# Fewer weight-sum transfers in the mixer's last stages, more in the MLP, and a last matrix part that reads all its weight sums from the scratch

## The chip, the cores and the metric

The kernel runs on one core of one Trainium2 chip. The metric is the device time of the whole program in microseconds (us), the median of several executions; lower is better. The five engines of the core are named as in the profile: PE (matmul; PEld is its weight load), DVE (vector), ACT (scalar), POOL (GpSimd) and SP (here only an issuer of transfers). ACT, POOL and SP each issue transfers on a queue of their own, and the 16 DMA engines of the core carry them.

## The reference, cut to what matters

Two layers, each a mixer (attention and mLSTM side by side) and then a squared-ReLU MLP, on 512 tokens of width 1024:

```python
h = rmsnorm(x, norm_mix); z = h @ w_in          # mixer: attention, mLSTM, gates
mixed = sigmoid(g_a) * (att @ w_att_branch) + sigmoid(g_m) * (hm @ w_m_branch)
x = x + mixed @ w_out
u = relu(rmsnorm(x, norm_ffn) @ w_ff1)          # MLP: 1024 -> 4096
x = x + (u * u) @ w_ff2                         #      4096 -> 1024
```

All of it is float32. The change touches how the weights of the MLP, `w_ff1` and `w_ff2`, reach the matmuls, and nothing that is computed.

## The kernel before, in words

**Matmuls in split precision.** Every operand is split into a high and a low part (`wh`, `wl` for weights, `uh`, `ul` for activations): ACT makes the high part by a copy that rounds, DVE subtracts it to get the low part. Three matmuls (`mm3`: high·high, high·low, low·high) stand for one.

**The MLP by Strassen's scheme.** The MLP is cut into four parts of 1024 hidden columns. Part 0 of the first matrix is done plainly (class `Plain`). The other products take seven block products in place of eight (numbered 1, 5, 6, 3, 7, 2, 4 in the order of work), with sums of weight blocks as operands. `first(part, i, u)` makes the hidden activations, `second(part, u)` multiplies them by `w_ff2` and adds the results to `x` (`gain`, one DVE instruction for each 128x512 block, reading a PSUM bank and freeing it). Each block product of `second` is a slot of two units (24 matmuls of 128x512 in all), each of `first` a slot of one unit; there are 102 units in a layer, in the order of the list `slots`, and the split weights are prepared `SPL` = 5 units ahead (`prepare`). Part 3's `second` comes last and has no `first` slots between its own.

**Weight sums by transfers.** The four sums that the scheme needs (D, A, B, C) can be made by the DMA engines in a scratch in DRAM: a "copy" (`Sums.copy`, issued by ACT, line 400) puts one block there, an "add" (`Sums.add`, issued by POOL, line 405) accumulates a second one onto it. B adds D, and C adds B, so these come later. Each copy and add moves half a matrix block, 512 KB. The scratch then holds the sum, and SP loads it like any weight. For `w_ff1` all four sums come this way; for `w_ff2` only D does, and `weights(which, h)` in `second` makes the others on the way with `plus` (DVE, line 925), in place on the loaded raw tile.

**When the transfers go out.** `plan_sums` lists the copies and adds of a layer as `jobs` (64 in a layer), and each `beat` takes the next job. Beats stand at fixed places of the mixer's stages (`beats(...)` beside `weave`), and in the MLP after units with `i % 5 in (1, 3)`. A copy is tied by `issue_after` to the last weight split on ACT; an add is tied to a small POOL copy (`mark`, line 403) that reads that split. The program's scheduler places them in the engines' instruction streams by these ties.

**Buffers around the change.** The loads of `second` go to four raw buffers (`raw2`, tags `p` and `q` for each half `h`); a load waits until the last reader of its buffer is done. Loads of `first` (`load1`, line 948) share three raw buffers. `w_m_branch`, the mixer's last but one weight, and `w_out`, its last, go through `chunk` (line 182 for the load, 192 and 193 for the split), with three raw buffers.

Of the kernel before, what the change touches and what calls it, by code (L numbers as in the profile page):

```python
# [19 lines left out]
D = 1024  # L20
KT = D // P
# [14 lines left out]
def hybrid_kernel(ctx, tc, x, norm_mix, w_in, att_q_norm, att_k_norm, att_sinks, m_gate_bias,  # L36
# [84 lines left out]
    def g_mix(l, k):  # L121
        return gcol[:, 8 * l + k:8 * l + k + 1]

    def g_ffn(l, k):
        return gcol[:, 16 + 8 * l + k:17 + 8 * l + k]
# [128 lines left out]
    def weave(fill, side=()):  # L254

        side = sorted(side, key=lambda e: e[0])
        at = 0.0
        for width, f in fill:
            while side and side[0][0] <= at + 1e-6:
                side.pop(0)[1]()  # L260
            f()
            at += width
        for _, f in side:
            f()
# [76 lines left out]
    norm = norm0 = Norm(lambda k: g_mix(0, k))  # L341
# [32 lines left out]
    jobs, sums = [], {}  # L374
# [38 lines left out]
    def plan_sums(l):  # L413

        s = [None] + [Sums(l, part, w1_rows) for part in range(1, 4)]
        p = [Sums(l, part, w2_rows, "D") for part in range(4)]
        sums.clear()
        sums.update({(1, part): s[part] for part in range(1, 4)})
        sums.update({(2, part): p[part] for part in range(4)})
        jobs.extend(s[1].copies("DABC") + s[1].adds("DAB") + p[0].copies("D") + s[1].adds("C")  # L420
                    + s[2].copies("DABC") + p[0].adds("D") + s[2].adds("DAB") + p[1].copies("D") + s[2].adds("C")
                    + s[3].copies("DABC") + p[1].adds("D") + s[3].adds("DAB") + p[2].copies("D") + s[3].adds("C")
                    + p[3].copies("D") + p[2].adds("D") + p[3].adds("D"))

    def beat():
        if jobs:
# [2 lines left out]
    def beats(*at):  # L429
        return [(a, beat) for a in at]  # L430

    def mixer(l, norm, late, order, phase):
# [319 lines left out]
        def ev_v(b, ps):  # L752
            if b == 0:
# [6 lines left out]
        side = [(0, lambda: k_vec(0)), (0, lambda: q_vec(0)), (0, lambda: k_vec(1)), (0, lambda: q_vec(1)),  # L760
                (7 - 1.25, lambda: k_tr(0)), (7 - 1.75, lambda: q_tr(0))]
# [100 lines left out]

        side += [(57.75 + 1.25 * f, lambda f=f: head_tr(f)) for f in range(MH)]
        plan_sums(l)
        side += beats(*(2.5 * n for n in range(1, 17)), *(42 + 1.5 * n for n in range(14)))
        weave(feat_steps(acts, wcols(C_QM, 512), ev_qk) + s0 + s1 + tok_steps(acts, wcols(C_VM, 512), ev_v)
              + a_steps(0, g0) + a_steps(1, g1) + s2 + tok_steps(acts, wcols(C_OM, 512), ev_o) + s3, side)
        sgm = [g2, g3]
# [1 line left out]
        for g in range(2):  # L870
            def ev_m(m, ps, g=g):
                i = 4 * g + m
                ve.tensor_tensor(sgm[g][m], sgm[g][m], ps, op=ALU.mult)
                ve.tensor_tensor(prod[i], prod[i], sgm[g][m], op=ALU.add)
                mixed[i] = split(prod[i])

            weave(feat_steps(hmT, lambda k, g=g: [w_m_branch[l, k * P:(k + 1) * P, 512 * g:512 * g + 512]], ev_m),
                  beats(1.0, 2.5))


        norm = Norm(lambda k: g_ffn(l, k))
# [10 lines left out]
    def mlp(l, norm, late, phase):  # L892
# [18 lines left out]
        def w_split(r):  # L911

            with tc.high_priority():
                hi, lo = (spl.tile(list(r.shape), F32R, tag=t, name=nm(t)) for t in ("wh", "wl"))
                last_wh[:] = sc.activation(hi, r, AF.Copy), hi[:, 0, :]  # L915
                ve.tensor_tensor(lo, r, f32(hi), op=ALU.subtract)  # L916
            return hi, lo
# [44 lines left out]
        def second(part, u):  # L962

            a11, a12, a21, a22 = (u[i][:, :, H * t:H * (t + 1)] for t in range(2) for i in range(2))
            s = uraw.tile([P, 4, H], F32, tag="s", name=nm("s"))
            end = part == 3
            b11, b12, b22, b21 = ([None] * 2 for _ in range(4))
            ps = {}

            def load(to, tag, h, src):  # L970
                with tc.high_priority():
                    to[h] = raw2.tile([P, 2, T], F32, tag=f"{tag}{h}", name=nm("raw"))
                    nc.sync.dma_start(to[h], src.rearrange("(k p) n -> p k n", p=P))

            def block(i, j, h):
                return w2_rows(l, part, i, j, h)

            def weights(which, h):
                if which == 1:
                    load(b11, "p", h, block(0, 0, h))  # L980
                    load(b12, "q", h, block(0, 1, h))
                    r = w_split(b11[h])
                    plus(b11[h], b11[h], b12[h])
                elif which == 5:
                    load(b22, "q", h, block(1, 1, h))
                    r = w_split(b11[h])
                    plus(b11[h], b11[h], b22[h])
                elif which == 6:
                    r = w_split(b11[h])
                elif which == 3:  # L990
                    r = w_split(b22[h])
                elif which == 7:
                    load(b12, "q", h, sums[2, part].to("D", h))
                    r = w_split(b12[h])
                elif which == 2:
                    load(b21, "q", h, block(1, 0, h))
                    r = w_split(b21[h])
                    plus(b21[h], b21[h], b11[h])
                else:
                    r = w_split(b21[h])  # L1000
                return r

            def left(which):
                if which == 5:
                    minus(s, a22, a21)
                elif which == 6:
                    minus(s, s, a11, -1.0)
                elif which == 3:
                    minus(s, s, a12, -1.0)
                elif which == 7:  # L1010
                    minus(a21, a11, a21)
                return {1: a11, 2: a12, 4: a22, 7: a21}.get(which, s)

            def slot(which, bank, fresh, gains):

                ws, a = {}, []

                def prep(h):
                    ws[h] = weights(which, h)

                def run(h):
                    if h == 0 and fresh:
                        ps[bank] = banks(bank)
                    (hi, lo), (ah, al) = ws[h], a[0]
                    for kt in range(2 * h, 2 * h + 2):
                        for i in range(2):
                            c = slice(i * P, (i + 1) * P)
                            mm3(ps[bank][:, i, :], ah[:, kt, c], al[:, kt, c], hi[:, kt % 2, :], lo[:, kt % 2, :],
                                fresh and kt == 0, False, skip_group_check=True)

                return Slot([lambda: prep(0), lambda: prep(1)], [lambda: run(0), lambda: run(1)],
                            lambda: [gain(t, j, ps[bank], g, d) for t, j, g, d in gains],
                            lambda: a.append(u_split(left(which))))

            x_, y_ = "xy" if part % 2 == 0 else "yx"
            z_ = "f" if end else y_
            return [slot(1, x_, True, [(0, 0, 1, False)]), slot(5, y_, True, [(1, 1, -1, False)]),
                    slot(6, x_, False, [(0, 1, -1, False)]), slot(3, y_, False, [(0, 1, -1, end)]),
                    slot(7, x_, False, [(1, 1, -1, end)]), slot(2, z_, True, [(0, 0, 1, end)]),
                    slot(4, x_, False, [(1, 0, 1, end)])]  # L1040
# [100 lines left out]
        class Plain:  # L1141
# [5 lines left out]
            def load(self, h):  # L1147
                self.w[h] = load1(w_ff1[l, T * h:T * (h + 1), self.c0:self.c0 + H])
# [21 lines left out]
        plain = [Plain(0, 0, "f"), Plain(0, 1, "x")]  # L1170
        for h in range(2):
            for f in plain:
                f.load(h)
        weave([(0.5, lambda k=k, f=f: f.step(k)) for k in range(KT) for f in plain], late + [(6.5, norm.inverse)])
        for f in plain:
            f.evac(us[0])
        us.append(new_u(1))
# [24 lines left out]
        def go(i, s, n):  # L1202
            if i == 0:
                s.before()
            prepare(i + SPL)
            at = slots.index(s) + 1
            if n == 0 and at < len(slots):
                slots[at].before()
            s.runs[n]()
            if n == len(s.runs) - 1:  # L1210
                s.done()
            if i % 5 in (1, 3):
                beat()

        weave([(1.0 if i >= len(units) - 4 else 0.0, lambda i=i, s=s, n=n: go(i, s, n))
# [3 lines left out]
    late = ([(0.75 + 0.9 * (k - 2), lambda k=k: norm.turn(k)) for k in range(2, KT)]  # L1219
            + [(6.5, lambda: gains(grow, 16))]  # L1220
            + [(3.0 + 2.0 * j, lambda j=j: norm.squares(j)) for j in range(2)])
    order = None
    for l in range(DEPTH):
        with ExitStack() as phase:
            norm = mixer(l, norm, late, order, phase)
        late = norm.steps(1, 1.5, 0.5)
        with ExitStack() as phase:
            norm = mlp(l, norm, late, phase)
        late = norm.steps(0, 1.5, 0.5) if norm else []
# [41 lines left out]
```

## Time and profile before

| | before |
|---|---|
| median of 3 executions | 1349.47 us (1347.91 to 4564.59) |
| profiled execution, whole | 1353.9 us |
| its span, first to last instruction | 1352.2 us |
| PE busy | 1307.2 us, 97% of the span |
| DVE busy | 970.2 us, 72% |
| ACT busy | 763.0 us, 56% |
| bytes moved by DMA | 219.58 MB |
| copies into the scratch / adds | 64 / 64, 512 KB each |

The page is read from PE outward: PE is busy nearly all of the span, so time can be lost only in its few gaps and where its clock is lower (the granted clock, 0.992 over the span). The other engines matter where PE waits for them. Windows of the span show where the gaps are; the chain that ended last and the waits show what ended them.

### The profile page before, as it was taken

The page shows a single profiled execution, that of the slowest core. Times are in us where ns is not written, and L with a number is a line of the kernel's source. Part 1 is how long each engine was busy: PE and PEld are TensorE (multiplying, and loading weights), DVE is VectorE, ACT ScalarE, POOL GpSimd, SP SyncE. Part 2 cuts the span into 40 slices and gives each one's busy share as a digit, 9 for nine tenths or more (in the row PEclk, how much of TensorE's full clock was granted, in tenths as well). Part 3 has the DMA queues.
Part 4 walks back from the last instruction along what each step waited for, and adds up shares of the span by engine and source line. Part 5 has one row for each costly group of instructions (what it writes and reads, how often), then busy time and mean ns, then how long its engine had stood idle before and what let it go on. Part 6 is the DMA issues. An engine that isn't in the chain of part 4 may idle for free. (4 is left out here: it accounts for less than half of the span.)

```text
span 1352.2 us, 19313 instructions
## 1 busy us (share of the span) xinstructions
PE 1307.2 (97%) x6966; PEld 1107.0 (82%) x6966; DVE 970.2 (72%) x1505; ACT 763.0 (56%) x1367; POOL 204.9 (15%) x347
## 2 busy tenths in 40 slices
PE   8999999979999999999999999999999999999998
PEld 6877788868889989998778777888788898898977
DVE  4688764566568797978847887645746678879796
ACT  5468765443366555666444687554534566665653
POOL 4423410110001111000005124102100021110000
PEclk9999999989999999999999999999999999999999
DMA  5544556987147969553225455568871489793523
GB/s 149 153 133 117 121 135 196 222 216 216 63 126 207 252 187 255 174 172 94 70 80 172 117 121 121 147 194 209 240 215 47 143 230 252 217 242 116 175 75 125
DMA packets 145473, 219.58 MB, mean 162 GB/s; under 512 B 11097, under 2 KB 66497, under 8 KB 145377
## 3 DMA queue, kind: packets, MB, share of 16 engines
q1 hardware_dynamic: 109600, 150.56, 36.0%
q0 software_dynamic: 17792, 33.69, 15.2%
q10 hardware_dynamic: 17984, 34.09, 8.0%
q8 instruction: 55, 0.90, 0.3%
q14 instruction: 42, 0.34, 0.1%
HBM read 216.21 MB, written 69.21 MB: 211 GB/s over the span
## 5 line engine op out<-in xcount | busy, mean ns | idle before, releaser
L47 PE MATMUL mm<-i,wh 128*128 128x512 f32 (+1 forms) x1280 | 353.9, 362 | 1.4 <-ACT kvi L463 0.9
L915 ACT ACTIVATE wh<-raw 128x1024 fp32r<-128x1024 f32 x212 | 222.3, 1054 | 168.5 <-PE mm L47 95.7
L916 DVE TENSOR_TENSOR wl<-raw,wh 128x1024 fp32r<-128x1024 f32 x212 | 257.3, 1221 | 74.9 <-ACT wh L915 74.7
L47 PEld LDWEIGHTS mm<-i,wh 128*128 128x128 f32 x1280 | 224.7, 189 | 34.7 <-ACT kvi L463 1.8
L193 DVE TENSOR_TENSOR wl<-w,wh 128x512 fp32r<-128x512 f32 (+1 forms) x208 | 143.0, 689 | 142.2 <-ACT wh L192 140.5
L47 PE MATMUL mm<-i,wl 128*128 128x512 f32 (+1 forms) x640 | 229.6, 359 | 0.0
L192 ACT ACTIVATE wh<-w 128x512 fp32r<-128x512 f32 (+1 forms) x208 | 127.1, 612 | 173.0 <-PE mm L47 113.0
L47 PE MATMUL mm<-wh,uh 128*128 128x512 f32 x448 | 176.5, 394 | 6.6 <-DVE x L957 6.6
L47 PE MATMUL mm<-wl,uh 128*128 128x512 f32 x448 | 176.2, 393 | 0.7 <-DVE wl L916 0.7
L47 PE MATMUL mm<-wh,ul 128*128 128x512 f32 x448 | 175.8, 392 | 0.0
L47 PE MATMUL mm<-wh,i 128*128 128x512 f32 (+1 forms) x512 | 151.6, 373 | 0.4 <-ACT wh L192 0.4
L403 POOL COPY mark<-wh 1x2 f32<-1x2 f32 x64 | 51.5, 804 | 613.9 <-ACT wh L915 399.1
L47 PEld LDWEIGHTS mm<-i,wl 128*128 128x128 f32 x640 | 120.9, 189 | 17.7
L47 PE MATMUL mm<-hs,wh 128*128 128x256 f32 x576 | 107.3, 287 | 3.7 <-ACT u L1103 3.6
L47 PEld LDWEIGHTS mm<-wh,i 128*128 128x128 f32 x512 | 92.9, 190 | 15.9 <-ACT wh L192 0.8
L47 PEld LDWEIGHTS mm<-wh,uh 128*128 128x128 f32 x448 | 85.1, 190 | 23.8 <-ACT uh L907 7.4
L47 PEld LDWEIGHTS mm<-hs,wh 128*128 128x128 f32 x576 | 90.0, 191 | 13.4 <-ACT u L1103 12.5
L47 PEld LDWEIGHTS mm<-wl,uh 128*128 128x128 f32 x448 | 85.1, 190 | 17.1 <-DVE wl L916 1.2
L47 PEld LDWEIGHTS mm<-wh,ul 128*128 128x128 f32 x448 | 84.8, 189 | 17.2 <-DVE ul L908 0.2
L47 PE MATMUL mm<-wl,i 128*128 128x512 f32 (+1 forms) x256 | 94.9, 371 | 0.0
L957 DVE SCALAR_TENSOR_TENSOR x<-mm,ninv,x 128x512 f32<-128x512 f32 x112 | 80.2, 745 | 12.5 <-PE mm L47 12.1
L47 PE MATMUL mm<-hs,wl 128*128 128x256 f32 x288 | 81.4, 283 | 0.0
(243 smaller groups left out, 2152.3 us busy)
## 6 DMA issues: line engine op xcount, KB each, us to landing
raw<-in_w_ff_dram SPq DMA_DIRECT2D x116, 512.0 KB, 5.6
w<-in_w_in_dram SPq DMA_DIRECT2D x128, 256.0 KB, 3.2
sum<-in_w_ff_dram ACTq DMA_DIRECT2D x64, 512.0 KB, 4.3
raw<-sum SPq DMA_DIRECT2D x64, 512.0 KB, 6.0
sum<-in_w_ff_dram POOLq DMA_DIRECT2D x40, 512.0 KB, 7.1
sum<-sum POOLq DMA_DIRECT2D x24, 512.0 KB, 6.2
w<-in_w_out_dram SPq DMA_DIRECT2D x32, 256.0 KB, 3.4
w<-in_w_att_branch_dram SPq DMA_DIRECT2D x16, 256.0 KB, 2.9
```

The lines of the kernel that those rows point to most:

```text
L47: return nc.tensor.matmul(*args, **kw)
L192: last_wh[:] = sc.activation(wh[:, :off], raw[:, :off], AF.Copy), wh
L193: ve.tensor_tensor(wl[:, :off], raw[:, :off], f32(wh[:, :off]), op=ALU.subtract)
L403: m = gp.tensor_copy(mark, f32(last_wh[1][0:1, 0:2]))
L915: last_wh[:] = sc.activation(hi, r, AF.Copy), hi[:, 0, :]
L916: ve.tensor_tensor(lo, r, f32(hi), op=ALU.subtract)
L957: ve.scalar_tensor_tensor(xh[:, i, :], ps[:, i, :], norm.inv[:, 0 if sign > 0 else 1, b:b + 1], xh[:, i, :], op0=ALU.mult, op1=ALU.add)
```

## The change

In the mixer the beats of the second stretch stand 2.0 apart in place of 1.5 and are 10 in place of 14; each half of the `w_m_branch` stage has one in place of two; the `w_out` stage keeps its 8. The plain start of the MLP gets four beats, and the MLP's units have a beat after every second one. The list of jobs gets the sums A, B and C of part 3 of `w_ff2`, so that a layer has 38 copies and 38 adds in place of 32 and 32 (and three empty jobs). In `second` for part 3, every weight is now loaded as it is used, from `w_ff2` or from the scratch, into the raw buffers p and q in turn, and the six `plus` of a layer in that part are gone.

```diff
     def plan_sums(l):
 ...
-        p = [Sums(l, part, w2_rows, "D") for part in range(4)]
+        p = [Sums(l, part, w2_rows, "D") for part in range(3)] + [Sums(l, 3, w2_rows)]
 ...
-                    + p[3].copies("D") + p[2].adds("D") + p[3].adds("D"))
+                    + p[3].copies("DABC") + p[2].adds("D") + p[3].adds("DAB") + [lambda: None] * 3 + p[3].adds("C"))
 ...
-        side += beats(*(2.5 * n for n in range(1, 17)), *(42 + 1.5 * n for n in range(14)))
+        side += beats(*(2.5 * n for n in range(1, 17)), *(42 + 2.0 * n for n in range(10)))
 ...
-                  beats(1.0, 2.5))
+                  beats(2.0))
 ...
             def weights(which, h):
+                if end:
+                    tag = "pqpqpqp"[(1, 5, 6, 3, 7, 2, 4).index(which)]
+                    plain = {1: (0, 0), 3: (1, 1), 2: (1, 0)}.get(which)
+                    load(b11, tag, h, block(*plain, h) if plain else
+                         sums[2, 3].to({5: "A", 6: "B", 7: "D", 4: "C"}[which], h))
+                    return w_split(b11[h])
 ...
-        weave([(0.5, lambda k=k, f=f: f.step(k)) for k in range(KT) for f in plain], late + [(6.5, norm.inverse)])
+        weave([(0.5, lambda k=k, f=f: f.step(k)) for k in range(KT) for f in plain], late + [(6.5, norm.inverse)] + beats(1.0, 3.0, 5.0, 7.0))
 ...
-            if i % 5 in (1, 3):
+            if i % 2:
                 beat()
```

**DVE at the start of part 3, first layer.** `wl` rows are weight splits, `L925` the sums made on DVE, `L930` and `L932` the activation sums, `ul` the low part of the activations, and the `x` rows are `gain`, reading a PSUM bank; `mm_5478` is the bank that part 2's last slot filled and that part 3's second slot needs. Before:

```order
L916 TENSOR_TENSOR wl_6189<-raw_6108,wh_6188 128x1024
L930 TENSOR_TENSOR s_3738<-u_3736,u_3735 128x1024
L925 TENSOR_TENSOR raw_6108<-raw_6108,raw_6186 128x1024
L930 TENSOR_TENSOR u_3735<-u_3735 128x4x256
L957 SCALAR_TENSOR_TENSOR x_0_122<-mm_5478,ninv_3704,x_0_122 128x512
L916 TENSOR_TENSOR wl_6212<-raw_6145,wh_6211 128x1024
L908 TENSOR_TENSOR ul_6236<-s_3738,uh_6235 128x1024
L925 TENSOR_TENSOR raw_6145<-raw_6145,raw_6209 128x1024
L932 SCALAR_TENSOR_TENSOR s_3738<-s_3738,u_3735 128x1024
L957 SCALAR_TENSOR_TENSOR x_0_120<-mm_6239,ninv_3704,x_0_120 128x512
L916 TENSOR_TENSOR wl_6231<-raw_6108,wh_6230 128x1024
L957 SCALAR_TENSOR_TENSOR x_0_122<-mm_5478,ninv_3704,x_0_122 128x512
```

The same place in the changed kernel (there the bank is `mm_5487`):

```order
L916 TENSOR_TENSOR wl_6204<-raw_6201,wh_6203 128x1024
L930 TENSOR_TENSOR s_3739<-u_3737,u_3736 128x1024
L930 TENSOR_TENSOR u_3736<-u_3736 128x4x256
L916 TENSOR_TENSOR wl_6226<-raw_6223,wh_6225 128x1024
L957 SCALAR_TENSOR_TENSOR x_0_122<-mm_5487,ninv_3704,x_0_122 128x512 x2
L908 TENSOR_TENSOR ul_6251<-s_3739,uh_6250 128x1024
L916 TENSOR_TENSOR wl_6246<-raw_6243,wh_6245 128x1024
L932 SCALAR_TENSOR_TENSOR s_3739<-s_3739,u_3736 128x1024
```

The `L925` rows are gone, and the two `gain` rows of the bank, seven places apart before, stand next to each other.

**ACT at the end of the `w_m_branch` stage, first layer.** `L192` rows split chunks of `w_m_branch` and then `w_out`, `L915` rows split the MLP's first weights, and `L400` rows issue copies; `wh_3154` is the split of the last `w_m_branch` chunk. Before:

```order
L915 ACTIVATE wh_3585<-raw_3583 128x1024
L192 ACTIVATE wh_3134<-w_3132 128x512
L915 ACTIVATE wh_3761<-raw_3759 128x1024
L192 ACTIVATE wh_3154<-w_3152 128x512
L203 ACTIVATE a_3070<-a_1400 128x512
L192 ACTIVATE wh_3198<-w_3196 128x512
L203 ACTIVATE a_3076<-a_1402 128x512
L400 DMA sum_628<-in_w_ff_dram 256x512
```

The same place in the changed kernel, where that split is `wh_3145`:

```order
L915 ACTIVATE wh_3580<-raw_3578 128x1024
L192 ACTIVATE wh_3127<-w_3125 128x512
L915 ACTIVATE wh_3762<-raw_3760 128x1024
L400 DMA sum_624<-in_w_ff_dram 256x512 x2
L192 ACTIVATE wh_3145<-w_3143 128x512
L203 ACTIVATE a_3063<-a_1403 128x512
L192 ACTIVATE wh_3189<-w_3187 128x512
```

Two copies (of `w_ff1`'s third sum D, jobs of the new beats in the MLP's plain start) now stand ahead of the split of the last `w_m_branch` chunk.

**POOL in the same stage.** Each add is one `L405` behind its `L403`; `sum_627` belongs to part 0 of `w_ff2`, `sum_619` to `sum_622` to the second sums of `w_ff1`. The two rows of `sum_621` before, and what stands at that place now:

```order
L403 COPY mark<-wh_3095 1x2
L405 DMA sum_621<-sum_620 256x512
L403 COPY mark<-wh_3134 1x2
L405 DMA sum_621<-sum_620 256x512
L403 COPY mark<-wh_3273 1x2
```

```order
L403 COPY mark<-wh_3107 1x2
L405 DMA sum_627<-in_w_ff_dram 256x512
L403 COPY mark<-wh_3189 1x2
L405 DMA sum_620<-in_w_ff_dram 256x512
L403 COPY mark<-wh_3228 1x2
```

Before, both adds are tied to splits of `w_m_branch` chunks (`wh_3095`, `wh_3134`). Now only one is (`wh_3107`), and the next one follows the split of a `w_out` chunk (`wh_3189`).

## The prediction

> **What bounds the kernel now.** I read the page's busy line, then what PE waited for, then windows around those waits, then the timelines of the engines that PE waited for.
>
> ```profile
> PE 1307.2 (97%) x6966; PEld 1107.0 (82%) x6966; DVE 970.2 (72%) x1505; ACT 763.0 (56%) x1367; POOL 204.9 (15%) x347
> ...
> PE mm L47 <- DVE a L873: 10.2, 2, 6.8
> PE mm L47 <- DVE x L957: 6.6, 2, 3.3
> ```
>
> PE is idle for only 1352.2 - 1307.2 = 45 us, so the change is decided in these 45 us and in stretches where PE runs at a lower clock. PE's two largest waits (us in total, times, longest) come once in each layer. The first lies in the `w_m_branch` stage, the second at the start of part 3 of `second`. The change touches both places, so each is followed to its cause.
>
> **The wait at part 3.** Windows of layer 0 (length; PE, PEld, DVE, ACT, POOL busy with counts; clock; DMA share; GB/s):
>
> ```profile
> 640.00:645.00 5.00, 1.70 (x7) 1.13 (x6) 5.00 (x7) 2.95 (x3) 0.00 (x0) 0.88 0.00 0
> 645.00:650.00 5.00, 5.00 (x18) 4.01 (x18) 4.57 (x5) 1.06 (x1) 0.00 (x0) 0.78 0.12 28
> 650.00:655.00 5.00, 5.00 (x24) 4.13 (x23) 4.60 (x5) 2.27 (x3) 0.00 (x0) 1.00 0.53 185
> ```
>
> PE loses 3.3 us while DVE is busy for all 5.00 us and DMA does nothing: DVE is the bound here. In the next window the granted clock is 0.78, and 18 matmuls run in place of 24. Layer 1 shows which DVE work it is: the DVE timeline, then two PE rows that are 28 matmuls apart, then the chain that ended last (start, us):
>
> ```profile
> 1303.11 1.22 DVE L925 TENSOR_TENSOR raw<-raw,raw 128x1024 f32<-128x1024 f32 x1
> 1304.25 1.22 DVE L930 TENSOR_TENSOR u<-u 128x1024 f32<-128x1024 f32 x1
> 1305.39 0.74 DVE L957 SCALAR_TENSOR_TENSOR x<-mm,ninv,x 128x512 f32<-128x512 f32 x1
> ...
> 1308.31 1.22 DVE L925 TENSOR_TENSOR raw<-raw,raw 128x1024 f32<-128x1024 f32 x1
> ...
> 1312.38 1.40 DVE L957 SCALAR_TENSOR_TENSOR x<-mm,ninv,x 128x512 f32<-128x512 f32 x2
> ...
> 1303.01 0.39 PE L47 MATMUL mm<-wh,uh 128*128 128x512 f32 x1
> ...
> 1309.36 0.39 PE L47 MATMUL mm<-wl,uh 128*128 128x512 f32 x1
> ...
> 1313.27 34.29 PE mm L47 x144
> ```
>
> PE's second slot of part 3 needs the bank that two `gain` instructions free. The first runs at 1305.39, the second only at 1312.38, because six DVE instructions stand between them (the DVE excerpt ahead), and PE starts again at 1313.27.
>
> **The wait in the `w_m_branch` stage.** SP, POOL and ACT rows of layer 0, then ACT's of layer 1:
>
> ```profile
> 276.15 2.64 SPq L948 DMA_DIRECT2D raw<-in_w_ff_dram  x3
> 279.03 0.34 SPq L182 DMA_DIRECT2D w<-in_w_m_branch_dram  x1
> ...
> 278.38 0.57 POOL L405 DMA_DIRECT2D sum<-sum  x1
> ...
> 282.56 0.79 POOL L405 DMA_DIRECT2D sum<-sum  x1
> ...
> 282.16 1.06 ACT L915 ACTIVATE wh<-raw 128x1024 fp32r<-128x1024 f32 x1 [0.33 <-DMA raw<-in_w_ff_dram]
> 291.66 0.63 ACT L192 ACTIVATE wh<-w 128x512 fp32r<-128x512 f32 x1 [8.44 <-DMA w<-in_w_m_branch_dram]
> ...
> 962.16 0.63 ACT L192 ACTIVATE wh<-w 128x512 fp32r<-128x512 f32 x1 [4.56 <-DMA w<-in_w_m_branch_dram]
> ```
>
> The last chunk of `w_m_branch` is issued at 279.03, behind three raw loads on its own queue and beside two adds on POOL's. ACT gets it at 291.66. PE's 6.8 us, and 10.2 - 6.8 = 3.4 us in layer 1, come from that.
>
> **The change part by part.** *Part 3, DVE.* Six `plus` (L925) a layer go, 1.22 us each by the row above (1.14 from start to start); four of them stand at the start of part 3, and the two `gain` rows of the bank move together. Replayed with these durations, `s` and `u` (L930) end by 1303.5 in place of 1305.4, and one split follows. Part 2's last slot ends on PE at about 1304.4, so both `gain` are done by about 1306. PE's own pace is (1309.36 - 1303.01) / 28 = 0.227 us a matmul, and its first slot of part 3 ends at 1309.8: the bank is there 3.8 us early. What is late next is the low part of the activations for the fourth slot, which the replay puts 0.5 us ahead of PE, so no new wait, but a narrow one. The gain is the idle 6.6 us of both layers and the slower clock behind it: in layer 0 (24 - 18) x 0.227 = 1.4 us, in layer 1 34.29 - 144 x 0.227 = 1.6 us. Together **-9.6 us**. The other two `plus` of a layer stand later, where PE has work; their end changes nothing.
>
> *Part 3, loads.* SP issues 14 loads a layer in place of 10. A load waits for the split four units earlier, 4 x 12 x 0.227 = 10.9 us ahead of its own split, and the DMA share in the windows above is 0.00 to 0.53. The page's landing time for such loads is 6.0 us (row below), so they are covered, with 4.9 us to spare; without cover each would cost PE what it is late.
>
> ```profile
> q1 hardware_dynamic: 109600, 150.56, 36.0%
> q0 software_dynamic: 17792, 33.69, 15.2%
> q10 hardware_dynamic: 17984, 34.09, 8.0%
> raw<-sum SPq DMA_DIRECT2D x64, 512.0 KB, 6.0
> ```
>
> *What a transfer costs.* Shares are of 16 engines' span (q1 is SP's queue, q0 POOL's, q10 ACT's). An add takes 0.152 x 1352.2 / 64 = 3.2 us of all 16 engines, a copy 0.080 x 1352.2 / 64 = 1.7 us, a raw load of 512 KB 0.360 x 1352.2 x 0.524 / 150.56 = 1.7 us.
>
> *The `w_m_branch` stage.* By the POOL excerpt, one add (the row at 278.38) stays beside the critical load and one (282.56) moves behind it: -3.2 us of DMA work. By the ACT excerpt, two copies now follow the L915 row at 282.16, ahead of the split that waits: +3.4 us at the same moment. Bounds: -3.2 us a layer if the copies come too late to matter, +3.4 us if the add did not matter; both terms are equally near to the load, so I take their difference, 0.2 us, as **0**. Issuing the two copies costs ACT nothing, since it idles 8.44 and 4.56 us there. The four earlier adds that leave this stretch cost nothing before, since PE does not wait there.
>
> By the Trainium skill (DMA: Bandwidth & Descriptors, section "Queues, rings and completion order"), each DMA engine goes round the queues that have work. Copies on a third queue would then take turns that SP's load had before; my estimate by that page is 0.7 us more a layer, and the sum below would be 1341.4. No row shows three queues busy at that place.
>
> *The `w_out` stage* keeps its 8 jobs, but six are adds where two were: 4 x (3.2 - 1.7) = 6 us more DMA work a layer. Two windows show its stretch:
>
> ```profile
> 300.00:325.00 25.00, 25.00 (x112) 20.71 (x111) 15.87 (x27) 8.30 (x14) 2.77 (x4) 1.00 0.73 193
> 325.00:350.00 25.00, 25.00 (x120) 20.73 (x119) 12.40 (x18) 8.25 (x17) 0.00 (x0) 1.00 0.55 175
> ```
>
> DMA has 25 x 0.27 + 25 x 0.45 = 18 us to spare there: **0**, and 6 us a layer if that room can't be used.
>
> *The MLP.* Each layer gets six more copies, six more adds and four loads, 6 x 1.7 + 6 x 3.2 + 4 x 1.7 = 36 us of DMA work, and the mixer's jobs move here too. Windows, then DMA shares and a wait in 415 to 475, and the first and last of eight adds:
>
> ```profile
> 425.00:450.00 25.00, 25.00 (x164) 22.95 (x164) 19.31 (x21) 16.35 (x20) 4.75 (x6) 1.00 1.01 261
> 550.00:575.00 25.00, 25.00 (x145) 21.88 (x144) 25.00 (x26) 15.45 (x18) 0.00 (x0) 1.00 0.41 127
> q1 hardware_dynamic: 7727, 9.96, 50.4%
> q0 software_dynamic: 2176, 4.19, 43.6%
> DVE raw L925 <- DMA raw<-in_w_ff_dram: 3.8, 2, 3.1
> ...
> 417.04 0.89 POOL L405 DMA_DIRECT2D sum<-in_w_ff_dram  x1
> ...
> 465.53 0.89 POOL L405 DMA_DIRECT2D sum<-sum  x1 [0.33 <-issue]
> ```
>
> DMA is full (1.01) from 425 to 450, and yet PE is busy for 25.00 of 25.00: loads are prepared five units ahead, and that covers the 3.1 us by which one was late. From the first of these adds to the last, 48.5 us, lie 17 units (beats after units 11 to 28): 2.9 us each. Adds come every 2 units in place of 2.5, so their share rises from 3.2 x 0.4 / 2.9 = 44% to 55%, beside 50% of loads: 5% too much, over eight adds (16 units, 46 us) 2.5 us of lateness. There are two such stretches a layer, so at most 4 x 2.5 = 10 us, at least nothing. It is nearest to the row in which 3.1 us did not reach PE, so I take **0**.
>
> *Sum.* -9.6 us on the profiled execution: 1353.9 becomes 1344.3 (span 1352.2 to 1342.6). That execution lies 4.4 us above the median of the runs, so for the median I forecast 1349.5 - 9.6 = **1340**.
>
> **The rivals.**
> - *The `w_m_branch` wait shrinks too.* If the copies matter less than the add, each layer gains up to 3.2 us: 1340 - 6.4, about 1333.5. For it: less is queued ahead. Against it: the place of the two copies.
> - *Loads come late where adds stand denser (the other side).* If SP's loads lose their lead beside the adds, the four MLP stretches cost 10 us and the two `w_out` stages 12 us: 1340 + 22 = 1362, slower than before. It decides once a load is later than the 3.1 us that PE did not feel. Against it: PE's 25.00 of 25.00 at a DMA share of 1.01.
> - *POOL's marks are locked out.* One mark took 4.84 us; the last row has least, median and most of all 64 (ns):
>
> ```profile
> 490.99 4.84 POOL L403 COPY mark<-wh 1x2 f32<-1x2 f32 x1 [24.57 <-ACT wh L915]
> ACT wh L915 <- POOL mark L403: 4.4, 2, 2.2
> L403 POOL COPY mark<-wh x64: 174/639/4840, 115.1 to 1205.7; 1x2 f32<-1x2 f32 x64
> ```
>
>   DVE was busy without a break then, and it is again from 550 to 575 (25.00), where about five more marks a layer now fall. An ACT split waited 2.2 us for a mark, twice. If each did and PE felt it, 5 x 2 x 2.2 = 22 us: 1362. Against it: the mark's buffer is needed again only five units, 14 us, later. The Trainium skill (SBUF — State Buffer, "Who interferes with whom") has the rule: a DVE instruction with two SBUF inputs blocks a GpSimd instruction that reads SBUF. The row at 490.99 agrees.
> - *Nothing is gained.* If another DVE result than the bank is late at part 3 (the replay's 0.5 us is narrow), the 9.6 us stay: 1349.5.
>
> **How the numbers follow.** Chances: forecast 0.60, `w_m_branch` shrinks 0.17, nothing gained 0.10, late loads 0.10, marks 0.03. The range 1331 to 1353 takes in the forecast, the first rival and the last, and most of the bounds of the `w_m_branch` stage (6.4 us either way); it leaves out late loads and marks, 0.13. About 2%, 27 us, is what a measurement of this kernel can tell from no change. Faster than that needs both PE waits gone and more, 0.03; slower needs more than any rival priced here, 0.02; within it 0.95.
>
> **What would show it.** In the profile after, PE's wait for `gain` (3.3 us, twice) is gone and the clock stays at 1.00 at the start of part 3; DVE's L925 rows fall by 12. ACT still waits several us for the last `w_m_branch` chunk in both layers. DMA share is higher from 425 to 600, and PE has no new wait for splits there. I am wrong if PE waits at part 3 for another instruction, if the `w_m_branch` wait moves by over 3 us in a layer, or if PE waits for splits inside the MLP.

## The result, and the profile after

The changed kernel takes **1339.58 us** (median of 4 executions, 1338.42 to 1341.12), beside 1350.79 us for the kernel before on the same chip; the ratio is 0.9925, with a 95% interval of 0.9901 to 0.9949. Measured again later, it took 1340.50 us beside 1351.53 (0.994, 0.9919 to 0.9961). The forecast was 1340. One of the four executions of the kernel before took 4564.59 us and is left out of the ratio. The 2% that the prediction gives as the least that can be told from no change is too coarse: the interval of this ratio is 0.5% wide.

The page's busy line of the changed kernel, and the largest waits of PE inside the layers (us in total, times, longest):

```profile
PE 1299.9 (97%) x6966; PEld 1101.6 (82%) x6966; DVE 957.3 (72%) x1493; ACT 763.1 (57%) x1367; POOL 225.3 (17%) x371
...
PE mm L47 <- DVE a L873: 7.0, 5, 2.8
PE mm L47 <- ACT u L1109: 5.5, 7, 1.0
```

DVE has 12 instructions fewer (1505 to 1493). PE's wait at part 3 for `gain` (L957, 6.6 us) is no longer in the list. The waits for L873, 10.2 us in two pieces before, both at the end of the `w_m_branch` stage, are 7.0 us in five, and 5.2 us of these lie at the start of `w_out`. L1109 is the line L1103 of before; that wait was 3.6 us.

**Part 3.** The windows of layer 0 that answer to those of the prediction, then DVE's rows at the start of part 3, then the last long piece of the chain that ended last:

```profile
640.00:645.00 5.00, 5.00 (x24) 4.14 (x23) 5.00 (x6) 2.59 (x4) 0.00 (x0) 1.00 0.40 126
645.00:650.00 5.00, 5.00 (x24) 4.14 (x23) 5.00 (x6) 2.80 (x3) 0.00 (x0) 1.00 0.84 227
650.00:655.00 5.00, 5.00 (x24) 4.14 (x23) 4.79 (x6) 3.07 (x3) 0.00 (x0) 1.00 0.23 87
```

```profile
627.77 1.23 DVE L930 TENSOR_TENSOR s<-u,u 128x1024 f32<-128x1024 f32 x1
629.03 1.22 DVE L930 TENSOR_TENSOR u<-u 128x1024 f32<-128x1024 f32 x1
630.18 1.22 DVE L916 TENSOR_TENSOR wl<-raw,wh 128x1024 fp32r<-128x1024 f32 x1
631.31 1.41 DVE L957 SCALAR_TENSOR_TENSOR x<-mm,ninv,x 128x512 f32<-128x512 f32 x2
```

```profile
1288.28 43.56 PE mm L47 x192
```

The two `gain` of the bank stand together at 631.31, one split behind the activation sums. PE runs 24 matmuls in each 5 us at a clock of 1.00, and in layer 1 192 matmuls without a gap, 43.56 / 192 = 0.227 us each. DVE is still busy for 5.00 of 5.00 us, so little room is left there.

**The `w_m_branch` stage.** ACT's rows of layer 0, then PE's waits there, the last row from layer 1 (start, us, and in brackets the idle time and what ended it):

```profile
282.57 1.23 ACTq L400 DMA_DIRECT2D sum<-in_w_ff_dram  x2
285.95 0.63 ACT L192 ACTIVATE wh<-w 128x512 fp32r<-128x512 f32 x1 [2.33 <-DMA w<-in_w_m_branch_dram]
...
294.58 0.63 ACT L192 ACTIVATE wh<-w 128x512 fp32r<-128x512 f32 x1 [3.94 <-DMA w<-in_w_out_dram]
```

```profile
287.96 0.74 PE L47 MATMUL mm<-a,wh 128*128 128x512 f32 x2 [0.99 <-DVE a L873]
297.29 0.47 PE L47 MATMUL mm<-wh,a 128*128 128x512 f32 x1 [1.74 <-DVE a L873]
...
959.94 0.51 PE L47 MATMUL mm<-wh,a 128*128 128x512 f32 x1 [2.79 <-DVE a L873]
```

ACT's wait for the last `w_m_branch` chunk fell from 8.44 to 2.33 us, but behind the two copies that ACT now issues at 282.57 a `w_out` chunk is late, by 3.94 us, which was not so in layer 0 before. In layer 1 PE's wait at the last `w_m_branch` chunk fell too, from 3.31 to 0.76 us, and the 2.79 us at the start of `w_out` took that back.

**Where the time went, by stages.** The starts of four kinds of PE rows cut an execution into stages: the first matmul of `w_m_branch`, the first four transposes of `x` at the end of `w_out`, the transposes at the layer change that wait for the last `gain`, and the end of the span. Lengths in us, each from one profiled execution, for all kernels of this study (the experiments that the names stand for follow):

| kernel | `w_m_branch`+`w_out`, layer 0 | MLP, layer 0 | mixer, layer 1, up to `w_m_branch` | `w_m_branch`+`w_out`, layer 1 | MLP, layer 1 |
|---|---|---|---|---|---|
| before | 57.2 | 352.1 | 264.5 | 53.0 | 353.2 |
| changed | 52.0 | 347.5 | 262.4 | 53.3 | 349.2 |
| changed, again | 53.8 | 346.8 | 262.4 | 52.2 | 350.7 |
| only the beats | 53.3 | 351.3 | 262.2 | 52.8 | 353.1 |
| only part 3 | 56.3 | 347.7 | 264.7 | 53.3 | 351.3 |
| four sums at the start | 52.8 | 353.1 | 262.2 | 53.6 | 358.8 |
| four sums later | 52.9 | 353.3 | 262.2 | 52.9 | 353.5 |
| no plain beats | 50.3 | 350.0 | 263.8 | 50.1 | 348.6 |
| raw loads behind `w_out` | 56.4 | 347.3 | 262.3 | 56.5 | 348.5 |
| the same, splits later, no plain beats | 58.4 | 344.0 | 263.8 | 62.3 | 350.6 |
| two sums in slot 2 | 53.2 | 346.4 | 262.7 | 55.9 | 353.3 |
| a beat every unit | 53.8 | 378.3 | 262.2 | 53.0 | 373.8 |
| wait filled | 54.0 | 350.3 | 262.2 | 56.3 | 350.7 |
| no plain or `w_m_branch` beats | 48.7 | 346.1 | 263.5 | 47.8 | 348.2 |

The sum of the changed kernel's differences, -15.6 us, is larger than the measured 11, since the profiled execution of before lay 3 us above its median and the changed one's 1 us below.

### The profile page after: what moved, and what is told of

Its sections match the earlier page's. It is cut to its first block, busy times and chain, and to the rows that moved or that the text cites. A ratio compares the mean times of both kernels' runs of the same rounds, so it can differ in the third digit from the quotient of the medians.

```text
span 1336.7 us, 19393 instructions
## 1 busy us (share of the span) xinstructions
PE 1299.9 (97%) x6966; PEld 1101.6 (82%) x6966; DVE 957.3 (72%) x1493; ACT 763.1 (57%) x1367; POOL 225.3 (17%) x371
## 5 line engine op out<-in xcount | busy, mean ns | idle before, releaser
L915 ACT ACTIVATE wh<-raw 128x1024 fp32r<-128x1024 f32 x212 | 222.4, 1053 | 151.6 <-PE mm L47 109.3
L192 ACT ACTIVATE wh<-w 128x512 fp32r<-128x512 f32 (+1 forms) x208 | 127.0, 612 | 163.0 <-PE mm L47 119.5
L403 POOL COPY mark<-wh 1x2 f32<-1x2 f32 x76 | 64.0, 843 | 713.0 <-ACT wh L915 481.4
L957 DVE SCALAR_TENSOR_TENSOR x<-mm,ninv,x 128x512 f32<-128x512 f32 x112 | 79.8, 745 | 16.2 <-PE mm L47 15.6
L47 PE MATMUL mm<-wh,a 128*128 128x512 f32 x256 | 82.9, 398 | 5.2 <-DVE a L873 5.2
```

What stands on the lines that cost most here:

```text
L47: return nc.tensor.matmul(*args, **kw)
L192: last_wh[:] = sc.activation(wh[:, :off], raw[:, :off], AF.Copy), wh
L403: m = gp.tensor_copy(mark, f32(last_wh[1][0:1, 0:2]))
L957: ve.scalar_tensor_tensor(xh[:, i, :], ps[:, i, :], norm.inv[:, 0 if sign > 0 else 1, b:b + 1], xh[:, i, :], op0=ALU.mult, op1=ALU.add)
```

## The experiments

**The two halves of the change.** The beats alone, on the kernel before:

```diff
-side += beats(*(2.5 * n for n in range(1, 17)), *(42 + 1.5 * n for n in range(14)))
+side += beats(*(2.5 * n for n in range(1, 17)), *(42 + 2.0 * n for n in range(10)))
-                  beats(1.0, 2.5))
+                  beats(2.0))
-... late + [(6.5, norm.inverse)])
+... late + [(6.5, norm.inverse)] + beats(1.0, 3.0, 5.0, 7.0))
-            if i % 5 in (1, 3):
+            if i % 2:
```

> The kernel before with only the transfers moved: the changed kernel's beats in the mixer, the plain stage and the MLP, while part 3 makes its sums on DVE as before and the list keeps its 64 jobs. Theory A (DVE's sums at the start of part 3 are what the change removes): PE still waits 3.3 us for the second gain in each layer, the clock is low behind it, and only the w_m_branch stage can give something: 1344 to 1351 us beside 1350. Theory B (the moved transfers carry the gain): about 1340, and the wait at part 3 is shorter by itself.

Measured: 1349.12 us beside 1351.17, ratio 0.9983 (0.9966 to 1.0), so 2.3 us less (0 to 4.6). PE's waits:

```profile
PE mm L47 <- DVE x L957: 6.6, 2, 3.3
PE mm L47 <- DVE a L873: 6.6, 5, 2.7
```

The wait for `gain` is as it was, and the `w_m_branch` waits are those of the changed kernel. Then part 3 alone, the changed kernel with the mixer's beats of before:

```diff
-side += beats(*(2.5 * n for n in range(1, 17)), *(42 + 2.0 * n for n in range(10)))
+side += beats(*(2.5 * n for n in range(1, 17)), *(42 + 1.5 * n for n in range(14)))
-                  beats(2.0))
+                  beats(1.0, 2.5))
-... + beats(1.0, 3.0, 5.0, 7.0))
+... )
```

> The changed kernel with the beats of the mixer as they were before (16, then 14 at 1.5, then 2 and 2, then 8; none in the plain stage); part 3 takes all its sums from the scratch, and the MLP keeps a beat after every second unit. Theory A: PE's wait at part 3 is gone, 8 to 10 us less than before, 1340 to 1342; PE still waits 10 us in all for the two last w_m_branch chunks. Theory B: 1348 to 1351. If the parts add up, this difference and that of the kernel with only the transfers moved together make that of the change.

Measured: 1344.65 us, ratio 0.9956 (0.9934 to 0.9977), so 5.9 us less (3.1 to 8.9).

```profile
PE mm L47 <- DVE a L873: 10.2, 2, 6.7
```

The wait for `gain` at part 3 is gone, the `w_m_branch` waits are those of before. Part 3 carries the larger share, less than the 8 to 10 us that theory A gave; 2.3 and 5.9 us make 8.2, which agrees with 10.1 (6.9 to 13.4) and 8.1 (5.3 to 10.9), the two measurements of the whole. In the profiled execution of part 3 alone one MLP load of layer 1 is late, and PE waits behind it. DVE's row, then PE's:

```profile
1216.94 1.22 DVE L925 TENSOR_TENSOR raw<-raw,raw 128x1024 f32<-128x1024 f32 x1 [6.22 <-DMA raw<-in_w_ff_dram]
...
1228.78 0.47 PE L47 MATMUL mm<-wh,uh 128*128 128x512 f32 x1 [1.09 <-DVE x L957]
1230.95 0.50 PE L47 MATMUL mm<-wl,uh 128*128 128x512 f32 x1 [1.70 <-DVE wl L916]
```

**Four sums back on DVE, at the start of part 3 and later.** The changed kernel, where the sums are made and thrown away:

```diff
-                    return w_split(b11[h])
+                    return (w_split(b11[h]), which in (1, 5) and plus(b11[h], b11[h], b11[h]))[0]
```

> The changed kernel with four DVE sums a layer put back at the start of part 3 (slots 1 and 5): each adds a block that has been split to itself, and nobody reads the sum. Same loads, same transfers. Theory A (DVE's time between the two gain instructions of the bank): the two gains come apart again, PE waits about 3 us for the second, twice, the clock drops behind it, and the time goes back up by 8 to 10 us, to 1348 to 1350. Theory B (the loads from the scratch or the moved transfers matter, not DVE): 1340 as the changed kernel.

Measured: 1352.30 us, ratio 1.0015 (0.9999 to 1.0032): the whole gain (10.1 and 8.1 us by the two measurements) is gone with loads and transfers unchanged, as theory A said. Windows of layer 0:

```profile
635.00:640.00 5.00, 1.70 (x6) 1.12 (x5) 5.00 (x7) 2.00 (x2) 0.00 (x0) 0.78 0.49 137
640.00:645.00 5.00, 5.00 (x14) 3.89 (x13) 3.93 (x4) 0.62 (x1) 0.00 (x0) 0.54 0.72 220
```

The same wait of 3.3 us as before, but with 14 matmuls in the 5 us behind it (18 in the kernel before) at a clock of 0.54. The same edit with `(7, 2)` in place of `(1, 5)`:

> The same four DVE sums a layer in the changed kernel, but in slots 7 and 2 of part 3, behind its third slot. Theory A (where the sums stand counts, not how many): no wait for a gain at the start of part 3, 1340 to 1342. Theory B (DVE is too busy over the whole of part 3): back up as with the sums at the start, 1346 to 1350.

Measured: 1351.93 us, ratio 1.0025 (1.0004 to 1.0046). Theory A falls in this point: the place does not spare them. DVE's rows and PE's wait show why:

```profile
653.66 1.22 DVE L925 TENSOR_TENSOR raw<-raw 128x1024 f32<-128x1024 f32 x1
654.80 0.74 DVE L957 SCALAR_TENSOR_TENSOR x<-mm,ninv,x 128x512 f32<-128x512 f32 x1
655.46 1.21 DVE L916 TENSOR_TENSOR wl<-raw,wh 128x1024 fp32r<-128x1024 f32 x1
656.59 1.22 DVE L908 TENSOR_TENSOR ul<-u,uh 128x1024 fp32r<-128x1024 f32 x1
```

```profile
657.86 0.52 PE L47 MATMUL mm<-wh,ul 128*128 128x512 f32 x1 [1.82 <-DVE ul L908]
```

The sums and the gains they pull apart stand ahead of the low part that the next slot needs. So at neither of the two places has DVE room for four sums. What of the two that the kernel before had in slot 2? The same edit with `(2,)`:

> The changed kernel with two DVE sums a layer put back in slot 2 of part 3, where the kernel before had its last two (each adds a block that has been split to itself, nobody reads the sum). The prediction costed these two at nothing. If that holds: no new wait of PE, 1339 to 1341. If DVE has no room there, PE waits for a low part (ul or wl) or a gain in each layer, 2 to 5 us in all with the clock: 1342 to 1345.

Measured: 1341.37 us, ratio 0.9935 (0.9915 to 0.9955), not to be told from the changed kernel. Windows of layer 1:

```profile
1315.00:1320.00 5.00, 5.00 (x24) 4.14 (x23) 5.00 (x6) 3.01 (x3) 0.00 (x0) 1.00 0.80 227
1320.00:1325.00 5.00, 5.00 (x24) 4.14 (x23) 5.00 (x6) 3.08 (x3) 0.00 (x0) 1.00 0.27 90
```

PE keeps its 24 matmuls and has no wait in part 3. The prediction's zero for these two holds within the measurement.

**What makes the weight chunks late.** The changed kernel without the plain stage's beats; near the chunks only the two copies at 282.57 go, the adds stay where they were:

```diff
-... late + [(6.5, norm.inverse)] + beats(1.0, 3.0, 5.0, 7.0))
+... late + [(6.5, norm.inverse)])
```

> The changed kernel without the four beats of the plain stage: those jobs go to the MLP's first units, so the two copies are no longer issued ahead of the last w_m_branch split, while the adds up to there stay. Theory C (the two copies, issued at 282.57 ahead of w_out's loads, cause the wait of 3.9 us for a w_out chunk and part of that for the last w_m_branch chunk): these waits shrink by about 3 us a layer, and the time falls by up to 6 us, to 1334 to 1338. Theory D (the adds alone set these waits, the copies do not matter): 1339 to 1341, with the waits as they are.

Measured: **1334.57 us**, ratio 0.9886 (0.9864 to 0.9907), theory C. ACT's rows of layer 0 and PE's waits of the stage:

```profile
285.64 0.63 ACT L192 ACTIVATE wh<-w 128x512 fp32r<-128x512 f32 x1 [2.92 <-DMA w<-in_w_m_branch_dram]
291.97 0.63 ACT L192 ACTIVATE wh<-w 128x512 fp32r<-128x512 f32 x1 [1.66 <-DMA w<-in_w_out_dram]
```

```profile
PE mm L47 <- DVE a L873: 3.4, 4, 1.6
```

The chunk of `w_out` is late by 1.66 us in place of 3.94, and PE waits 3.4 us in place of 7.0; the wait for the `w_m_branch` chunk stays. The copies came too late to hold up that chunk, which had been issued at 279.15; they held up the `w_out` chunk issued at 286.11. Next, the changed kernel with the MLP's first raw loads behind four chunks of `w_out` on SP:

```diff
-                nc.sync.dma_start(raw[:, off:off + n], s)
+                last_w[0] = nc.sync.dma_start(raw[:, off:off + n], s)
 ...
-                f.load(h)
+                with tc.issue_after(<the fourth w_out chunk's load>): f.load(h)
```

> The changed kernel with the MLP's first raw loads, which SP issued between the w_m_branch chunks, held back until four chunks of w_out are issued. Theory E (the raw loads ahead on SP's own queue make the last w_m_branch chunk and the first w_out chunks late): ACT's waits for them fall below 1 us in both layers, PE's 7 us of waits there go, 1332 to 1335. Theory D (the adds on POOL's queue make them late): the waits stay at 2 us and more, 1339 to 1341. If the held-back loads now make the plain stage wait, PE shows it there and the time rises.

Measured: 1347.86 us, ratio 0.9977 (0.996 to 0.9993). Theory E is right on the wait and wrong on the time: PE has no wait left up to 298, past the last `w_m_branch` chunk, but a longer one follows. (The copies, tied to the raw splits, move to 303.41 with them; the last `w_m_branch` chunk is late without copies too, by 2.92 us, so it is the move of the raw loads that took its wait away.) ACT's rows, then PE's wait:

```profile
300.61 1.06 ACT L915 ACTIVATE wh<-raw 128x1024 fp32r<-128x1024 f32 x1 [2.39 <-DMA raw<-in_w_ff_dram]
301.57 0.61 ACT L203 ACTIVATE a<-a 128x512 fp32r<-128x512 f32 x1
303.40 1.06 ACT L915 ACTIVATE wh<-raw 128x1024 fp32r<-128x1024 f32 x1 [1.21 <-DMA raw<-in_w_ff_dram]
```

```profile
303.58 0.79 PE L47 MATMUL mm<-wl,a 128*128 128x512 f32 x1 [4.80 <-DVE wl L193]
```

The splits of the raw tiles (L915) stand in ACT's stream between those of `w_out`; now they wait for their own loads, and `w_out` waits behind them. To take that away, the splits were put behind two chunks of the second `w_out` half too, with the plain beats left out:

```diff
-                f.load(h)
+                with <load behind w_out chunk 4, splits behind chunk 2 of the second half>: f.load(h)
 ...
-... + beats(1.0, 3.0, 5.0, 7.0))
+... )
```

> The changed kernel without the plain stage's beats, and with the MLP's first raw loads behind four chunks of w_out as in the kernel that only held these back, but now their splits on ACT and DVE stand behind two chunks of the second w_out half, so a raw load that lands late does not hold up a w_out split. If the wait of 4.8 us for wl in each layer came from ACT's order alone, the waits for w_m_branch and w_out (3.4 us with only the plain beats gone) go too: 1329 to 1333. If the raw loads late in the w_out stage make w_out's chunks or the plain stage late whatever the order: 1336 to 1345.

Measured: 1348.68 us, ratio 0.999 (0.9972 to 1.0008): above both expected ranges, so the order of the splits alone was not it. DVE's rows of layer 1, and PE's wait:

```profile
984.83 0.68 DVE L885 TENSOR_TENSOR x<-x,mm 128x512 f32<-128x512 f32 x1
992.27 1.23 DVE L916 TENSOR_TENSOR wl<-raw,wh 128x1024 fp32r<-128x1024 f32 x1 [6.76 <-ACT wh L915]
```

```profile
996.50 0.69 PE L51 MATMUL aux<-ident,x 128*128 128x128 f32 x2 [6.61 <-DVE x L885]
```

Now DVE waits 6.76 us for a raw split, and the last L885, which PE needs, stands behind it. So in both orders the late raw loads hold up something that PE needs; issued early, they do not.

Last, the beats that issue adds beside the critical chunk. On top of the kernel without plain beats:

```diff
             weave(feat_steps(hmT, lambda k, g=g: [w_m_branch[...]], ev_m),
-                  beats(2.0))
+                  ())
```

> The changed kernel without the plain stage's beats and without the two of the w_m_branch stage, so that neither the copies nor those two adds are issued near the last w_m_branch chunk; all jobs behind come one or two beats later. Theory D (an add beside the chunk still costs it time): ACT's waits of 2.6 to 2.9 us for the last w_m_branch chunk fall by up to 3.2 us, PE's 0.7 and 1.6 us there go, 1331 to 1334. Theory E (only the raw loads ahead on SP's queue are left as a cause): the waits stay, 1334 to 1336. If the later jobs reach part 2 or 3 late: new waits for wl there and 1337 or more.

Measured: **1329.73 us**, ratio 0.9829 (0.9805 to 0.9854), the fastest kernel of the study, 23 us below the kernel before. ACT's row and two windows:

```profile
286.16 0.64 ACT L192 ACTIVATE wh<-w 128x512 fp32r<-128x512 f32 x1 [1.13 <-DMA w<-in_w_m_branch_dram]
```

```profile
275.00:300.00 25.00, 24.95 (x111) 20.32 (x109) 22.18 (x32) 14.70 (x21) 3.19 (x4) 1.00 0.79 216
940.00:965.00 25.00, 25.00 (x111) 20.48 (x110) 22.41 (x35) 12.18 (x20) 5.00 (x7) 1.00 0.93 234
```

Theory D, and a little more than it gave: the chunk is late by 1.13 us in place of 2.92, which ACT's lead covers, and PE runs through the stage at a clock of 1.00. By the table the two adds cost 1.6 and 2.3 us in this stage; what else lies between 1334.57 and 1329.73 is not shown to be theirs (in the profile of the former PE waits some 3.5 us more in the MLP of layer 0). The kernels of this section agree in one point: raw loads, copies and adds, on three different queues, each cost a chunk time if they are queued when it is issued.

**How dense may the adds stand?** The changed kernel with a beat after every unit of the MLP:

```diff
-            if i % 2:
+            if True:
```

> The changed kernel with a beat after every unit of the MLP in place of every second one: the same 79 jobs, but adds follow each other at 2.7 us, less than the 3.2 us that one takes of the DMA engines, beside loads of about half. Theory F (loads come late where adds stand denser, once a load is later than the 3.1 us that PE did not feel): DMA share above 1 over tens of us, ACT and DVE wait 5 us and more for raw, PE for splits, 1350 to 1365. Theory G (five units of lead cover it): 1339 to 1342.

Measured: 1393.96 us, ratio 1.0309 (1.0286 to 1.0332). PE's largest wait, a window of layer 0 and ACT's rows in it:

```profile
PE mm L47 <- ACT u L1109: 40.0, 8, 9.5
```

```profile
450.00:475.00 25.00, 14.98 (x88) 13.73 (x89) 12.42 (x12) 7.88 (x11) 0.00 (x0) 0.80 0.96 293
```

```profile
457.14 1.06 ACT L915 ACTIVATE wh<-raw 128x1024 fp32r<-128x1024 f32 x1 [4.73 <-DMA raw<-in_w_ff_dram]
...
463.17 1.06 ACT L915 ACTIVATE wh<-raw 128x1024 fp32r<-128x1024 f32 x1 [4.97 <-DMA raw<-sum]
...
464.13 0.58 ACT L1109 ACTIVATE u<-mm 128x512 f32<-128x512 f32 x1
```

Theory F, and more than it gave. The `u` that PE waits for stands in ACT's stream behind splits that wait for their loads. So the rival of late loads is a real mechanism: with a beat every unit it costs tens of us, with one every two units at most a few, as in the profile of part 3 alone.

**What the slower clock costs.** The kernel before, with 14 matmuls that nobody reads in the place of PE's wait at part 3:

```diff
+                    fill = aux() if end and which == 1 and h else None
+                    [pe.matmul(fill, ah[:, 0, 0:P], hi[:, 0, :], start=True, stop=True) for _ in range(14) if fill is not None]
                 return Slot([lambda: prep(0), lambda: prep(1)], ...
```

> The kernel before with 14 extra matmuls (slot 1's own operands into a free bank that nobody reads) behind slot 1 of part 3, 14 x 0.227 = 3.2 us: as long as PE's wait for the second gain there. They take nothing of the wait away and put work in its place. Theory H (the slower clock behind the wait is a price of the idle time, and comes on top of it): no idle time of 3.3 us at part 3, the clock stays at 1.00 there, and the time falls by what the clock took, 2 x 1.5 = 3 us, more where the clock falls deeper: 1346 to 1348 beside 1350. Theory I (the clock has nothing to do with that wait): the clock falls as before and the time is 1350.

Measured: 1346.33 us, ratio 0.9966 (0.995 to 0.9982), so 4.6 us less (2.4 to 6.8) with the wait filled and not shortened. Windows of layer 0:

```profile
635.00:640.00 5.00, 4.88 (x22) 3.76 (x21) 5.00 (x6) 1.54 (x2) 0.00 (x0) 1.00 0.00 0
640.00:645.00 5.00, 5.00 (x24) 4.14 (x23) 4.82 (x6) 2.59 (x3) 0.00 (x0) 1.00 0.26 94
```

Theory H: with PE busy the clock stays at 1.00. Finally the changed kernel itself once more:

> The changed kernel once more, beside the others on the same chip: 1338 to 1342 beside 1350, and 4 to 6 us above the kernel without the plain stage's beats. Its profile should again show no wait for a gain at part 3 and the waits for w_m_branch and w_out chunks near 2 to 3 us; where its runs differ, the lower clock goes with the longer time.

Measured: 1340.50 us (1338.20 to 1348.85). Its profile again has no wait at part 3, and PE waits 7.4 us for L873. Its ten executions had mean clocks of 0.992 to 0.998, the longest (1348.85) the lowest; the 33 of the kernel before beside the first experiments ran from 1344.91 us at 0.995 to 1360.75 at 0.989.

## Why the prediction was right, point by point

- **Part 3, DVE (-9.6 us).** The mechanism is shown: the wait goes when the sums go, and comes back with four sums and nothing else. The size depends on how it is taken: part 3 alone gave 5.9 us (3.1 to 8.9), with a late load in its profile; the two MLP stages of the changed kernel are 4.6 and 4.0 us shorter, 8.6 in sum; and the four sums put back into the changed kernel cost 10 to 12 us by the ratios. Inside the term the clock's share, 3.0 us, agrees with the 4.6 (2.4 to 6.8) that filling the wait gave. It was read from one execution, and the price of one and the same 3.3 us differs: behind each wait the matmuls start 0.43 us apart in place of 0.227 for 3.0 us in the kernel before, and for 5.7 us in the one with four sums at the start, which costs 1.4 and 2.7 us.
- **Part 3, loads (0).** Held: the changed kernel has no wait of PE in part 3.
- **The two later sums (0).** Held, within the measurement. But the prediction's reason, that PE has work there, is weaker than it reads: four sums there cost the whole gain.
- **The `w_m_branch` stage (0).** Here the working failed, and the total hid it. The term was a difference of an add less (-3.2) and two copies more (+3.4) at the same moment. Both are real, but they hit different chunks: the chunk of `w_m_branch` came 5.7 us earlier in layer 0 (285.95 in place of 291.66), and the copies made the one of `w_out` behind it late. Layer 0 gained 5.2 us, layer 1 nothing (57.2 to 52.0, 53.0 to 53.3). So the rival in which this wait shrinks too came true, and the sign that the prediction named for being wrong, over 3 us in a layer, appeared in layer 0. The gain of both layers together is the firmer number: the three kernels with the mixer's beats of before have 109.6 to 110.3 us in these stages, the changed kernel 105.3 and 106.0. How it falls to the layers is not: PE's two waits are 6.84 and 3.31 us in the profile of before, and 3.40 and 6.43 with the wait at part 3 filled. What decides that is open.
- **The copies' price by the page.** The prediction's estimate from the Trainium skill (DMA: Bandwidth & Descriptors, "Queues, rings and completion order"), that each DMA engine goes round the queues that have work, was 0.7 us a layer. The trace agrees that transfers on another queue delay SP's load; the kernel without plain beats puts the copies at some 2.5 us a layer (52.0 and 53.3 us in the table against 50.3 and 50.1).
- **The `w_out` stage (0).** The free 18 us were a mean over windows of 25 us. The room was there, but not at 286 to 294, when the chunk was on its way. PE waited 1.74 us there, and 2.79 us in layer 1.
- **The MLP (0).** Nearly held in the changed kernel: the wait for ACT's `u` rose from 3.6 to 5.5 us, not the 10 us of the bound. DMA's share reached 1.05 from 425 to 450, and PE was busy for 24.71 of 25.00:

```profile
425.00:450.00 25.00, 24.71 (x154) 22.11 (x153) 17.81 (x18) 14.34 (x17) 6.24 (x8) 1.00 1.05 266
```

  But the prediction's footing for it was weak. It took the load that was 3.1 us late as one that PE did not feel, from a window (425 to 450) that ends before it. DVE's row of the kernel before, and PE's wait for the split that came late behind it:

```profile
469.57 1.22 DVE L925 TENSOR_TENSOR raw<-raw,raw 128x1024 f32<-128x1024 f32 x1 [3.12 <-DMA raw<-in_w_ff_dram]
...
484.30 0.50 PE L47 MATMUL mm<-wl,uh 128*128 128x512 f32 x1 [0.66 <-DVE wl L916]
```

  So that load reached PE, with 0.66 us; with part 3 alone, and the beats of the changed kernel in the MLP's units, one 6.22 us late cost 2.8 us. That is the rival of late loads in small.
- **The marks on POOL.** ACT's waits for a mark stayed at 5.2 us in all (4.4 before); that rival did not come.
- **Not in the sum.** The mixer of layer 1 became 2.1 us shorter. Its idle time at the layer change is the same (2.1 us), but the clock behind it stayed at 1.00, where it was 0.69 before. In the table the eight kernels with beats in the plain stage have 262.2 to 262.7 there, and five of the six without them 263.5 to 264.7; the sixth, the one with the wait filled, has 262.2. So the plain stage's beats may be what keeps the clock up, from one execution of each kernel; how they would, and why the sixth differs, is open.

So the mechanism of part 3 was right, but that the total came out at 1340 is in part luck: the `w_m_branch` stage, counted at nothing, gave 2 to 5 us, and part 3 from 4 us less than counted to 2 us more, as the measurements have it.

## What to carry to other kernels

Read a stall by the instruction that stands late in the stream of the engine that is waited for, and add the clock behind it to its price: here 4.6 us (2.4 to 6.8) on top of 6.6. Price transfers beside a critical load by what is queued on every queue when that load is issued, chunk by chunk, not by the mean share of a window. And where a load comes early to an engine that works in order, its early place is what protects the work behind it: moved late, it made first ACT and then DVE block.

## What was not expected of the hardware

- A wait's price in clock is not fixed, and it is large: behind the same 3.3 us at part 3, the clock was low for 3.0 us in one profile and for 5.7 us in another. Filling two such waits with matmuls that nobody reads saved 4.6 us (2.4 to 6.8).
- Shorter waits lower the clock as well. In the kernel with four sums at the start, PE waited 2.68 us for a `w_out` chunk of layer 0, and the clock was 0.66 around it:

```profile
295.00:300.00 5.00, 3.52 (x9) 2.81 (x10) 5.00 (x10) 1.59 (x3) 1.08 (x2) 0.66 0.89 160
```

The Trainium skill (TensorE: Matmul & The Clock Gate, "What's actually happening") has the clock at half after an idle window of some 3.4 us whose start does not follow the kernel. The traces agree with a half (matmuls 0.43 us apart in place of 0.227) and with a price that changes between executions; the 2.68 us show that less than the page's figure is enough, at least at times.
